# Weights split four units ahead, an input's own steps hurried alone, and new step numbers for a twelve-part transformer forward pass

## The chip, the cores and the metric

The kernel runs on one core of a Trainium2 chip. The metric is the time of one execution on the device in microseconds; of the kernel before, three runs gave 1786.06, 1789.84 and 1791.72 us, median 1789.84 us. TensorE does the matrix products, VectorE (DVE) and ScalarE (ACT) the element-wise work, GpSimd (POOL) a little of it, and SyncE (SP) issues nearly all DMAs.

## The reference, cut to what matters

The input is 256 tokens of 1024 float32 features. Four layers come first, each `x = x + m @ w_o` and then `x = x + ffn(rmsnorm(x))`, where m is an attention over `rmsnorm(x)`: differential attention in layers 0 and 3 (two softmaxes per head, subtracted, then a norm over the head's 128 features and a product with the values), stick-breaking attention in layer 1, sliding-window attention with sinks in layer 2. The feed-forward part is `(silu(gate) * val) @ w_down`, where gate and val come out of a 3-tap causal convolution over `h @ w_up`. A norm follows, and a second block: a SwiGLU feed-forward, a mixer (MoBA attention, which with 256 tokens is plain causal attention with ALiBi, beside a multi-scale pooling path), a cross-attention to 256 memory rows, and a second SwiGLU. Each branch of the second block is normed before and after:

```python
h = rmsnorm_2(x, mix_pre_g[l])
...
y = jnp.concatenate([attn, pool], axis=-1) @ w_out[l]
x = x + rmsnorm_2(y, mix_post_g[l])
```

## The kernel before, in words

**Weights.** All weight matrices lie in device memory as one stream in the order of use: blocks of 128x128, 8 blocks to a unit, two units to a 1 MB chunk, 564 units in all. SyncE loads a chunk into one of four `stage` buffers (`dma_to`, L124). A unit is split into a high part, rounded to the fast float32 format by ScalarE (`whi`, L162), and a low part, the rest, by VectorE (`wlo`, L165). There are five buffers for each part (`wsp`, L104). TensorE multiplies high weights by the high and by the low part of the input, and low weights by the high part: three matmuls of 256 columns to a block (`fm`, L187).

**The clock of the program is the block.** `self.pos` counts blocks. When `take` (L168) reaches the fifth block of unit u, it has the units up to u + AHEAD split, with AHEAD = 3 throughout (L115); the low part's instruction is issued `lag` blocks after the high part's. Everything that is not a weight product is a Python generator in `self.side` (`spawn`, L227). Each `yield n` puts its next step n blocks later, and `tick` (L231), called after every block, issues the steps that are due. The order in which the engines get their instructions is therefore written out by hand, in the numbers of `PLAN`, `MIX_PLAN`, `XA_STEPS`, `PACE`, `NORM_AT`, `V_AT`, `POST_AT`, `LAG` and `WARM`. Each engine works through its own instructions in that order and waits for the others by semaphores.

**Hurrying.** Where a weight product needs an input tile whose steps have not been issued yet (`kt not in act.done`, L191), it calls `tick(True)`, which issues the next step of every generator at once, whatever it belongs to, until the tile's steps are issued. `drain` (L239) does so until no generator is left.

**Attention layers** (`attn_layer`, L683). For each of 8 heads or blocks, q and k come from one unit each. `q_parts` and `k_parts` make the doubled high and low parts: a copy over 128x512 (L414, L433), and after `q[1]` or `k[1]` blocks the low parts on VectorE (L419, L437) and two copies over 64x256 (L438). The head's generator (`da_head`, `sb_block`, `sm_block`) starts `steps[0]` blocks after its k unit and then waits until both are issued (`parts_made`). The first numbers of `k` and `q` are the delay before the copy, `q_hi`, `k_hi` and `k_lo` say which engine copies (V or A). `out_proj` (L371) follows; the last head's steps are in `last`.

**Norms.** `feed` (L357) makes a tile of the next part's input (high part and square on ScalarE, low part and the sum of squares on VectorE). `start_norm` (L322) waits until all eight squares are summed, sums over partitions with a product by ones (L301), and makes 1/rms as `ln` and `exp` on ScalarE. The scale is applied to what comes out of the next weight product, so that product needs only the tiles of `feed`.

**Second block** (`body`, L1313). Between the first SwiGLU and the mixer stand 8 units that make the memory's keys (`mem_units(0, 8)`), 64 blocks, and beside them `post_apply` (L930) norms the branch, adds it to x and feeds the mixer's input tiles, one every PACE blocks from block POST_AT. Then comes `self.drain()` (L1357), and only then the mixer. The memory's values (`mem_units(8, 16)`, another 64 blocks) stand in the same way before the cross-attention. Before the second SwiGLU nothing stands between; 20 products of constants (`WARM`, L938) fill TensorE while the branch's norm is made.

Of the kernel before, what the change touches and what calls it, by code (L numbers as in the profile page):

```python
# [32 lines left out]
    dict(steps=(15, 7, 7, 2, 7, 4, 10, 2, 12, 11, 3), last=(9, 17, 5, 0, 1, 1, 6, 9, 5, 5, 7), q=(0, 2), k=(11, 5),  # L33
         q_hi="V", k_hi="A", k_lo="AA"),
    dict(steps=(14, 9, 3, 4, 4, 9, 2), last=(17, 8, 1, 8, 4, 9, 2), q=(2, 8), k=(2, 3), q_hi="A", k_hi="V", k_lo="AV"),
    dict(steps=(13, 8, 5, 4, 11, 8), last=(15, 8, 4, 0, 6, 2), q=(2, 8), k=(1, 8), q_hi="A", k_hi="A", k_lo="AA",
         norm="VVAA"),
    dict(steps=(14, 17, 9, 0, 9, 3, 9, 2, 9, 2, 7), last=(18, 7, 10, 1, 4, 0, 4, 11, 4, 1, 6), q=(2, 2), k=(3, 3),
         q_hi="A", k_hi="V", k_lo="AA"),
]  # L40
MIX_PLAN = dict(steps=(7, 13, 4, 6, 14, 1), last=(6, 17, 9, 10, 4, 7), norm="VVVV")
XA_STEPS = (0, 14, 2, 0)


PACE = dict(mix=10, xa=5, ffn2=6)
NORM_AT = (29, 11, 16, 10)
V_AT = (4, 5, 4, 6)
POST_AT = (3, 7)
LAG = (5, 7, 8, 6)
WARM = 20  # L50
# [42 lines left out]
class Net:  # L93
# [93 lines left out]
    def fm(self, specs, act, kts, first=True, last=True, rows=None, wide=False):  # L187
        ah, al = act.h, act.l
        for kt in kts:
            rw = rows[kt] if rows is not None else np.arange(128 * kt, 128 * kt + 128)  # L190
            while kt not in act.done:  # L191
                self.tick(True)
# [34 lines left out]
    def spawn(self, gen, delay=0):  # L227

        self.side.append([self.pos + delay, gen])

    def tick(self, force=False):  # L231
        for item in list(self.side):
            if item in self.side and (force or item[0] <= self.pos):
                try:
                    item[0] = self.pos + next(item[1])
                except StopIteration:
                    self.side.remove(item)
# [119 lines left out]
    def feed(self, act, j, g, split=True):  # L357
# [11 lines left out]
        self.spawn(low(), 1)  # L369
# [313 lines left out]
    def attn_layer(self, layer, xt):  # L683
# [4 lines left out]
        self.lag = LAG[layer]  # L688
        with ExitStack() as st:
# [9 lines left out]
            if mixer == 2:  # L699
# [7 lines left out]
                def block(b, ps):  # L707
# [3 lines left out]
                    self.spawn(self.sm_block(pool, oT, b, q, kk[b // 4], vget, sk, nxt, b == 7), plan[0])  # L711
# [8 lines left out]
            else:  # L720
# [17 lines left out]
                for h in range(8):  # L738
# [14 lines left out]
                    self.spawn(head, self.plan["last" if h == 7 else "steps"][0])  # L753
# [6 lines left out]
    def ffn_layer(self, layer, xf, nxt):  # L760
# [3 lines left out]
        with ExitStack() as st:  # L764
# [9 lines left out]
            self.lag = 6  # L774
            self.start_norm(delay=27)
# [47 lines left out]
            def start(n, i, bank, delay=0):  # L823
                gen = gate(n, i, bank)
                if delay:
                    self.spawn(gen, delay)
                else:
                    self.spawn(gen, next(gen))
# [34 lines left out]
    def swiglu(self, tag, xt, rget, down):  # L863

        nc = self.nc
        with ExitStack() as st:
# [36 lines left out]
            for i in range(22):  # L903
                if i < 2:
                    self.spawn(gate(i, lead[i]), 7 * i)
                else:
# [4 lines left out]
                    self.spawn(gen, next(gen))  # L911
# [549 lines left out]
```

## Time and profile before

| what | value |
|---|---|
| median of three runs | 1789.84 us |
| the profiled execution's own time | 1785.74 us |
| its span, first to last instruction | 1784.0 us |
| TensorE matmul busy | 1750.8 us (98%) |
| TensorE weight loads busy | 1636.8 us (92%) |
| VectorE busy | 1403.2 us (79%) |
| ScalarE busy | 1115.0 us (62%) |
| GpSimd busy | 27.1 us (2%) |
| mean granted TensorE clock over the span | 0.996 |

The busy time of a matmul is counted from its start to the modelled end of its way through the array, so neighbours overlap and a short wait between two of them hides in the overlap; a view that lists waits gives the part that is left over. Stages by time: start-up to 14 us, layer 0's attention to 143, its feed-forward part to 323, layer 1 to 628, layer 2 to 892, layer 3 to 1190, first SwiGLU to 1378, memory keys to 1402, mixer to 1492, memory values to 1515, cross-attention to 1580, second SwiGLU to the end.

### The profile page before, as it was taken

Reading aid. Unit: us, or ns where it says so; the run is one execution under the profiler, and the core shown is the slowest. Engines: PE = TensorE matmul, PEld = TensorE weight load, DVE = VectorE, ACT = ScalarE, POOL = GpSimd, SP = SyncE. Lnnn points to the kernel's source line nnn. Section 1 sums busy time; section 2 is a strip of 40 time slices with the busy share of each in tenths; the row PEclk is TensorE's granted clock in tenths of the full one; section 3 lists DMA queues with packets and bytes.
Section 4 is the critical chain, followed back from the end, with each engine's and each line's share of the span. In section 5 each row is a group of like instructions: output and inputs, shape, how many; then the busy total and the mean of one; then the engine's idle time right before and its main releaser. Section 6 shows DMA issues by size and latency. Waiting matters only on the chain.

```text
span 1784.0 us, 31555 instructions
## 1 busy us (share of the span) xinstructions
PE 1750.8 (98%) x12564; PEld 1636.8 (92%) x12564; DVE 1403.2 (79%) x2574; ACT 1115.0 (62%) x2004; POOL 27.1 (2%) x67
## 2 busy tenths in 40 slices
PE   8999999999999999999999999999999999999998
PEld 7899998999999899999899999988888889988886
DVE  6888996797998687998689799778865767558764
ACT  6676664676766477766467666556655456466653
POOL 1000000000000000000000000000000020000000
PEclk9999999999999999999999999999999999999999
DMA  8734555434455544455554355555555444345451
GB/s 276 253 136 169 190 186 200 155 142 164 156 190 201 198 154 165 149 189 187 201 189 151 146 189 190 189 195 182 190 189 189 166 154 166 120 153 186 172 212 68
DMA packets 56212, 314.66 MB, mean 176 GB/s; under 512 B 5616, under 2 KB 18320, under 8 KB 20224
## 3 DMA queue, kind: packets, MB, share of 16 engines
q1 hardware_dynamic: 54720, 309.79, 48.4%
q0 software_dynamic: 768, 2.09, 0.4%
q8 instruction: 99, 1.62, 0.4%
q10 hardware_dynamic: 576, 0.75, 0.1%
q14 instruction: 49, 0.40, 0.1%
HBM read 311.52 MB, written 5.29 MB: 178 GB/s over the span
## 4 chain that ended last, share of the span: by engine, by line
PE 79%; DVE 12%; ACT 5%; DMA 2%; issue 2%; DVEq 0%; ACTq 0%; SPq 0%
PE u L183 68%; PE s L183 10%; DVE wlo L165 3%; DMA stage<-w 1%; DVE y L797 1%; ACT whi L162 1%; DVE s L472 1%; ACT s L263 1%; DMA bt<-bt_d 1%; DVE qs L419 1%; PE s L489 0%; ACT ln L263 0%; DVE klow L437 0%; DVE u L886 0%; DVE u L883 0%
## 5 line engine op out<-in xcount | busy, mean ns | idle before, releaser
L183 PE MATMUL u<-xt,whi 128*128 128x256 f32 (+1 forms) x4352 | 863.0, 295 | 1.4 <-DVE xt L278 0.8
L165 DVE TENSOR_TENSOR wlo<-stage,whi 128x1024 fp32r<-128x1024 f32 (+1 forms) x568 | 680.3, 1213 | 73.1 <-ACT whi L162 72.1
L183 PEld LDWEIGHTS u<-xt,whi 128*128 128x128 f32 x4352 | 691.8, 192 | 21.2 <-issue 3.2
L183 PE MATMUL u<-xt,wlo 128*128 128x256 f32 x2352 | 666.1, 283 | 5.4 <-DVE wlo L165 5.4
L162 ACT ACTIVATE whi<-stage 128x1024 fp32r<-128x1024 f32 (+1 forms) x568 | 581.6, 1041 | 32.7 <-PE u L183 27.9
L183 PEld LDWEIGHTS u<-xt,wlo 128*128 128x128 f32 x2352 | 450.7, 192 | 7.0 <-DVE wlo L165 6.7
L183 PE MATMUL u<-ghl,whi 128*128 128x512 f32 x880 | 304.8, 389 | 0.0
L183 PE MATMUL u<-ghl,wlo 128*128 128x256 f32 x880 | 244.4, 279 | 0.0
L183 PEld LDWEIGHTS u<-ghl,whi 128*128 128x128 f32 x880 | 164.9, 187 | 37.8
L797 DVE SCALAR_TENSOR_TENSOR y<-ub,vec,y 128x256 f32<-128x256 f32 x344 | 159.5, 482 | 10.3 <-ACT y L793 3.3
L183 PEld LDWEIGHTS u<-ghl,wlo 128*128 128x128 f32 x880 | 165.0, 188 | 0.0
L183 PE MATMUL u<-o,whi 128*128 128x256 f32 x768 | 142.9, 286 | 0.1
L793 ACT ACTIVATE y<-ub,vec 128x256 f32<-128x256 f32 x172 | 94.2, 594 | 59.6 <-DVE ub L787 59.6
L183 PE MATMUL s<-xt,whi 128*128 128x512 f32 x352 | 128.1, 398 | 0.0
L183 PEld LDWEIGHTS u<-o,whi 128*128 128x128 f32 x768 | 118.7, 189 | 1.8 <-issue 1.2
L360 ACT ACTIVATE xt<-x,vec 128x256 fp32r<-128x256 f32 x72 | 36.4, 506 | 119.1 <-DVE x L846 89.9
L183 PE MATMUL u<-o,wlo 128*128 128x256 f32 x384 | 108.2, 282 | 0.0
L183 PE MATMUL s<-xt,wlo 128*128 128x256 f32 x352 | 99.9, 284 | 2.0 <-DVE wlo L165 1.7
L813 ACT ACTIVATE ghl<-g 128x256 fp32r<-128x256 f32 x88 | 36.9, 419 | 90.4 <-DVE g L809 88.5
L183 PE MATMUL u<-whi,xt 128*128 128x256 f32 (+1 forms) x448 | 90.0, 299 | 0.0
L263 ACT ACTIVATE s<-s,nm 128x128 f32<-128x128 f32 x112 | 49.7, 445 | 52.2 <-DVE nm L477 51.7
L183 PEld LDWEIGHTS s<-xt,whi 128*128 128x128 f32 x352 | 66.3, 188 | 15.5
(236 smaller groups left out, 2049.5 us busy)
## 6 DMA issues: line engine op xcount, KB each, us to landing
stage<-w SPq DMA_DIRECT2D x280, 1024.0 KB, 4.8
bt<-bt_d SPq DMA_DIRECT2D x24, 256.0 KB, 5.3
bt_d<-rows_d SPq DMA_DIRECT2D x1, 2048.0 KB, 12.3
stage<-w SPq DMA_DIRECT2D x4, 256.0 KB, 7.0
stage<-w SPq DMA_DIRECT2D x2, 512.0 KB, 9.0
bt_d<-rows_d SPq DMA_DIRECT2D x2, 512.0 KB
bt_d<-rows_d SPq DMA_DIRECT2D x1, 1024.0 KB
mem<-memT POOLq DMA_DIRECT2D x8, 128.0 KB, 2.6
```

Of the source, the lines that this page charges most:

```text
L162: nc.scalar.activation(hi[:, s], src[:, s], AF.Copy)
L165: nc.vector.tensor_tensor(lo[:, s], src[:, s], hi[:, s].bitcast(F32), OP.subtract)
L183: self.nc.tensor.matmul(out, lhsT, rhs, start=start, stop=stop, skip_group_check=True)
L263: self.nc.scalar.activation(out, in_, func, **kw)
L360: nc.scalar.activation(act.h[:, j], src, AF.Copy, scale=gcol)
L419: nc.vector.tensor_tensor(qs[other, j], q[own], qs[own, j].bitcast(F32), OP.subtract)
L472: nc.vector.tensor_tensor_reduce(s[:, j, sl], ps[j][:, sl], bt[:, j, bs], 1.0, init(j), OP.add, OP.max, mx[:, 2 * j + t:2 * j + t + 1])
L793: nc.scalar.activation(y[:, p], u[:, p, 2:258], AF.Identity, scale=cv(i, p, 2), bias=cv(i, p, 3))
L797: nc.vector.scalar_tensor_tensor(y[:, p], u[:, p, tap:tap + T], cv(i, p, tap), y[:, p], op0=OP.mult, op1=OP.add)
L813: nc.scalar.activation(gh[:m, i], g[:m], AF.Copy)
```

## The change: what it does

AHEAD becomes 4 in layers 1 to 3, in every feed-forward part and from there to the end; layer 0's attention keeps 3. A generator can be spawned with the input (`act`) that it makes, and where a product needs a tile of that input, `tick(act)` issues early the steps of that input's generators alone; the others stay at their due block. The two `drain` calls before the mixer and the cross-attention go, and `start_norm` gets a wait after the sums (0 and 4 blocks). The step numbers are new; layer 0's become nearly those of layer 3, including the engines of the two high copies.

```diff
 PLAN = [
-    dict(steps=(15, 7, 7, 2, 7, 4, 10, 2, 12, 11, 3), last=(9, 17, 5, 0, 1, 1, 6, 9, 5, 5, 7), q=(0, 2), k=(11, 5),
-         q_hi="V", k_hi="A", k_lo="AA"),
-    dict(steps=(14, 9, 3, 4, 4, 9, 2), last=(17, 8, 1, 8, 4, 9, 2), q=(2, 8), k=(2, 3), q_hi="A", k_hi="V", k_lo="AV"),
-    dict(steps=(13, 8, 5, 4, 11, 8), last=(15, 8, 4, 0, 6, 2), q=(2, 8), k=(1, 8), q_hi="A", k_hi="A", k_lo="AA",
-         norm="VVAA"),
-    dict(steps=(14, 17, 9, 0, 9, 3, 9, 2, 9, 2, 7), last=(18, 7, 10, 1, 4, 0, 4, 11, 4, 1, 6), q=(2, 2), k=(3, 3),
+    dict(steps=(14, 15, 11, 0, 9, 0, 9, 2, 9, 2, 12), last=(18, 7, 9, 1, 4, 1, 7, 11, 5, 1, 6), q=(2, 6), k=(5, 2),
+         q_hi="A", k_hi="V", k_lo="AA"),
+    dict(steps=(14, 9, 3, 7, 4, 9, 2), last=(17, 8, 1, 8, 4, 9, 2), q=(2, 8), k=(2, 5), q_hi="A", k_hi="V", k_lo="AV"),
+    dict(steps=(13, 8, 6, 4, 11, 8), last=(15, 8, 6, 0, 8, 2), q=(2, 8), k=(1, 8), q_hi="A", k_hi="A", k_lo="AA",
+         norm="VVAV"),
+    dict(steps=(14, 15, 11, 0, 9, 3, 9, 2, 9, 1, 12), last=(18, 7, 9, 1, 4, 0, 7, 11, 5, 1, 6), q=(2, 4), k=(6, 2),
          q_hi="A", k_hi="V", k_lo="AA"),
 ]
-MIX_PLAN = dict(steps=(7, 13, 4, 6, 14, 1), last=(6, 17, 9, 10, 4, 7), norm="VVVV")
-XA_STEPS = (0, 14, 2, 0)
-PACE = dict(mix=10, xa=5, ffn2=6)
-NORM_AT = (29, 11, 16, 10)
-V_AT = (4, 5, 4, 6)
-POST_AT = (3, 7)
-LAG = (5, 7, 8, 6)
-WARM = 20
+MIX_PLAN = dict(steps=(7, 13, 9, 7, 19, 1), last=(6, 17, 9, 10, 2, 7), norm="VVVV")
+R_WAIT = (0, 4)
+AHEAD = (3, 4, 4, 4)
+XA_STEPS = (0, 13, 3, 6)
+PACE = dict(mix=13, xa=8, ffn2=3)
+NORM_AT = (24, 12, 16, 11)
+V_AT = (6, 5, 4, 6)
+POST_AT = (4, 3)
+LAG = (9, 7, 8, 9)
+WARM = 12
...
             while kt not in act.done:
-                self.tick(True)
+                self.tick(act)
...
-    def spawn(self, gen, delay=0):
-        self.side.append([self.pos + delay, gen])
+    def spawn(self, gen, delay=0, act=None):
+        self.side.append([self.pos + delay, gen, act])
     def tick(self, force=False):
         for item in list(self.side):
-            if item in self.side and (force or item[0] <= self.pos):
+            if item in self.side and (force is True or item[0] <= self.pos or force and item[2] is force):
...
-        self.spawn(low(), 1)
+        self.spawn(low(), 1, act)
...
         self.lag = LAG[layer]
+        self.AHEAD = AHEAD[layer]
...
             self.lag = 6
+            self.AHEAD = 4
...
-                self.spawn(self.post_apply(xm, "mix_pre_g_2", PACE["mix"]), POST_AT[0])
-                self.start_norm(0.125, True)
+                self.spawn(self.post_apply(xm, "mix_pre_g_2", PACE["mix"]), POST_AT[0], xm)
+                self.start_norm(0.125, True, wait=R_WAIT[0])
                 self.mem_units(0, 8)
-                self.drain()
...
-                self.spawn(self.post_apply(xx, "xa_pre_g_2", PACE["xa"]), POST_AT[1])
-                self.start_norm(1.0 / 16)
+                self.spawn(self.post_apply(xx, "xa_pre_g_2", PACE["xa"]), POST_AT[1], xx)
+                self.start_norm(1.0 / 16, wait=R_WAIT[1])
                 self.mem_units(8, 16)
-                self.drain()
...
-            self.spawn(self.post_apply(xl, "ffn2_pre_g_2", PACE["ffn2"], True))
+            self.spawn(self.post_apply(xl, "ffn2_pre_g_2", PACE["ffn2"], True), 0, xl)
```

The heads, the gates of the feed-forward parts and the pooling groups are spawned with their own input in the same way.

## Rows read from the trace of the kernel before

**Rows 1.** Waits by engine, whole span: total us, times, longest us.

```profile
PE u L183 <- DVE wlo L165: 5.4, 5, 1.2
ACT whi L162 <- PE u L183: 27.9, 18, 2.4
```

**Rows 2.** Weight loads' waits, whole span, same columns.

```profile
PEld s L183 <- DVE wlo L165: 4.4, 8, 1.2
```

**Rows 3.** Busy us of engines in stretches: PE, PEld, DVE, ACT, POOL; clock; DMA.

```profile
30.00:143.00 113.00, 106.15 (x845) 102.85 (x844) 95.42 (x248) 77.13 (x179) 0.17 (x3) 1.00 0.59 207
892.00:1010.00 118.00, 117.58 (x955) 115.86 (x955) 100.92 (x251) 84.35 (x190) 0.16 (x3) 1.00 0.47 167
...
160.00:180.00 20.00, 20.00 (x169) 20.00 (x168) 19.30 (x33) 13.59 (x22) 0.00 (x0) 1.00 0.54 193
...
1240.00:1260.00 20.00, 19.44 (x108) 16.26 (x107) 16.75 (x30) 13.72 (x28) 0.54 (x1) 1.00 0.57 199
```

**Rows 4.** TensorE's waits in layer 0's attention, 30 to 143 us.

```profile
PE s L183 <- ACT ks L403: 3.8, 6, 0.9
PE s L183 <- DVE klow L437: 3.0, 4, 1.2
```

**Rows 5.** Chain that ended last, in order of time: start us, us, what.

```profile
42.59 12.94 DMA bt<-bt_d
```

**Rows 6.** VectorE in order of time, start of layer 0's feed-forward part.

```profile
152.25 1.21 DVE L165 TENSOR_TENSOR wlo<-stage,whi 128x1024 fp32r<-128x1024 f32 x1
...
156.61 1.22 DVE L165 TENSOR_TENSOR wlo<-stage,whi 128x1024 fp32r<-128x1024 f32 x1
```

**Rows 7.** TensorE's waits, 1190 to 1378 us (first SwiGLU).

```profile
PE s L183 <- DVE wlo L165: 1.7, 5, 0.9
```

**Rows 8.** TensorE's waits, 1378 to 1415 us, before the mixer.

```profile
PE s L183 <- DVE accss L295: 2.8, 1, 2.8
PE s L351 <- ACT r L263: 1.0, 1, 1.0
```

**Rows 9.** VectorE in order of time beside the memory keys: one round.

```profile
1389.36 0.41 DVE L943 TENSOR_TENSOR f<-f,r 128x256 f32<-128x256 f32 x1
1389.81 0.42 DVE L944 TENSOR_TENSOR x<-x,f 128x256 f32<-128x256 f32 x1
1390.15 0.48 DVE L364 SCALAR_TENSOR_TENSOR xt<-x,vec,xt 128x256 fp32r<-128x256 f32 x1
1390.55 0.41 DVE L295 TENSOR_TENSOR accss<-accss,sq 128x256 f32<-128x256 f32 x1
1390.88 1.22 DVE L165 TENSOR_TENSOR wlo<-stage,whi 128x1024 fp32r<-128x1024 f32 x1
1392.02 0.41 DVE L1055 TENSOR_TENSOR mK<-u,r 128x256 f32<-128x256 f32 x1
```

**Rows 10.** Engines in stretches, columns as in Rows 3.

```profile
1407.00:1410.30 3.30, 3.30 (x17) 3.30 (x18) 2.19 (x3) 2.18 (x3) 0.00 (x0) 0.51 0.00 0
1584.20:1587.20 3.00, 2.93 (x10) 2.48 (x11) 2.02 (x6) 2.06 (x4) 0.00 (x0) 0.56 0.00 0
```

**Rows 11.** In order of time, before the mixer: ones product, then scales.

```profile
1405.18 0.70 PE L183 MATMUL s<-accss,ones 128*128 128x256 f32 x2 [2.78 <-DVE accss L295]
...
1406.87 0.42 ACT L333 ACTIVATE rq<-r 128x256 f32<-128x256 f32 x1
```

**Rows 12.** TensorE's waits, 1495 to 1523 us, before the cross-attention.

```profile
PE s L183 <- DVE accss L295: 1.2, 1, 1.2
```

**Rows 13.** TensorE in order of time, before the second SwiGLU.

```profile
1580.92 2.53 PE L183 MATMUL s<-ones_r 128*128 128x128 f32 x20
1584.27 0.56 PE L183 MATMUL u<-xt,whi 128*128 128x512 f32 x1 [0.81 <-DVE xt L278]
```

**Rows 14.** Groups of instructions by form, layer 2, 628 to 711 us.

```profile
L633 ACT ACTIVATE s<-s,rs 128x256 f32<-128x256 f32 x8 | 4.0, 502 | 0.0
L635 DVE TENSOR_SCALAR s<-s,rs 128x256 f32<-128x256 f32 x8 | 2.8, 348 | 0.0
```

More of the change, by code (lines that the diff above doesn't have):

```diff
@@ L710, in block @@
                     plan = self.plan["last" if b == 7 else "steps"]
-                    self.spawn(self.sm_block(pool, oT, b, q, kk[b // 4], vget, sk, nxt, b == 7), plan[0])
+                    self.spawn(self.sm_block(pool, oT, b, q, kk[b // 4], vget, sk, nxt, b == 7), plan[0], oT)
                 rows = [np.concatenate([np.arange(64 * h, 64 * h + 64) for h in SW_HEADS[b]]) for b in range(8)]
@@ L752, in attn_layer @@
                         pool, oT, h, q, k, vget)
-                    self.spawn(head, self.plan["last" if h == 7 else "steps"][0])
+                    self.spawn(head, self.plan["last" if h == 7 else "steps"][0], oT)
                     if h // 2 not in vs and h in (0, 2, 4, 7):
@@ L824, in start @@
                 gen = gate(n, i, bank)
[L825 to L828, printed above, removed]
+                self.spawn(gen, delay or next(gen), ga)
             self.fm([(b[:, p * T:p * T + T], name, layer, cols, p == 0)
@@ L904, in swiglu @@
                 if i < 2:
-                    self.spawn(gate(i, lead[i]), 7 * i)
+                    self.spawn(gate(i, lead[i]), 7 * i, ga)
                 else:
@@ L910, in swiglu @@
                     gen = gate(i, outs)
-                    self.spawn(gen, next(gen))
+                    self.spawn(gen, next(gen), ga)
             down(ga)
@@ L1028, in finish @@
                 while kt not in act.done:
-                    self.tick(True)
+                    self.tick(act)
                 if h == 0 or kt < 18:
@@ L1103, in mix @@
                 p, q, k = self.units("w_in_2", 0, [1536 + c, c, 512 + c], xt)
-                self.spawn(self.pool_group(pool, oT, b, p))
+                self.spawn(self.pool_group(pool, oT, b, p), 0, oT)
                 q = self.scaled(pool, q, self.rq, "q", 3)
@@ L1107, in mix @@
             else:
-                self.spawn(self.pool_group(pool, oT, b, self.unit("w_in_2", 0, 1536 + c, xt)))
+                self.spawn(self.pool_group(pool, oT, b, self.unit("w_in_2", 0, 1536 + c, xt)), 0, oT)
                 q = self.scaled(pool, self.unit("w_in_2", 0, c, xt), self.rq, "q", 3)
@@ L1111, in mix @@
             plan = self.plan["last" if b == 3 else "steps"]
-            self.spawn(self.sm_block(pool, oT, b, q, k, vget, None, nxt, b == 3), plan[0])
+            self.spawn(self.sm_block(pool, oT, b, q, k, vget, None, nxt, b == 3), plan[0], oT)
             if b % 2:
@@ L1160, in xa @@
             q = [self.scaled(pool, p, self.rq, "q", 5) for p in ps]
-            self.spawn(self.xa_head(pool, oT, h, q), XA_STEPS[0])
+            self.spawn(self.xa_head(pool, oT, h, q), XA_STEPS[0], oT)
     def prelude(self, small):
```

## The prediction, made before the result was known

> **What bounds the kernel now.** I read the waits of TensorE first, because its matmuls are busy for 98% of the span: what the change can win is what TensorE waits for, and the list is short. The largest entries by place are low weight parts that come late, five times, 5.4 us [rows 1]; the same in the first SwiGLU's second bank, where the weight loads show 4.4 us [rows 2]; the parts of k in layer 0's attention, 6.8 us [rows 4]; and the norm before the mixer, 3.8 us [rows 8]. The stretches came next. In layer 3's attention TensorE is busy for 117.58 of 118 us, in layer 0's, with the same kind of heads, for 106.15 of 113 [rows 3]: layer 0 has idle time that layer 3 has not. In the middle of a feed-forward part 169 matmuls fill 20 us [rows 3], so a matmul of 256 columns takes 0.118 us and a block of three 0.355 us; I turn steps into time with that. There TensorE is at its pace and no order of steps helps.
>
> **The change part by part.** *AHEAD 4 in the feed-forward parts.* A split now takes the place that the previous unit's split had in the queues of ScalarE and VectorE, 8 blocks or 2.8 us earlier. At the start of layer 0's feed-forward part the low part that TensorE waits for begins at 156.61; the split one place earlier began at 152.25 [rows 6], 4.4 us before, and the wait is 1.1 to 1.2 us. So one place covers it. There is one such wait in each of the four convolution parts and a smaller one in the second SwiGLU, together the 5.4 us of [rows 1]. VectorE's work stays the same, so what is late next is the split after it, with the same lead. I take 5.0 us off, between 2 and 5.4.
>
> In the first SwiGLU the waits repeat: 1.7 us in TensorE's list [rows 7], 4.4 us in that of the weight loads [rows 2], in which the overlap with the matmul before is not hidden. VectorE is busy there for 16.75 of 20 us [rows 3], not full, so this is a backlog and not a rate, and 2.8 us more lead covers most of it. I take 3.0 us, about the middle, between 0 and 4.4.
>
> What this edit adds is a wait. Five buffers hold the high parts; a split four units ahead needs the buffer of the unit just finished, that is, TensorE must have come to 4 blocks before the split's place in the order, where it was 12 before. Behind the split in ScalarE's queue stand evacuations, gates and the copies of the heads, and VectorE waits for those. Today 18 of the 564 splits wait for TensorE, 27.9 us in all [rows 1], on an engine that is idle for a third of the span. I cost the edit at 0, because what stands behind a split mostly needs a product that is issued at about the same block; if that cover is missing it is the slow rival below. The loads of chunks are also queued by the splits, 8 blocks earlier on SP, and still wait for a stage buffer.
>
> *Layer 0's steps.* Now k's low parts are issued 16 blocks after k, and the scores right behind them, so TensorE arrives while ScalarE and VectorE are still copying: 3.8 and 3.0 us [rows 4]. With k=(5, 2) they are issued 7 blocks after k and the scores after 14: 7 blocks, 2.5 us, against 0.9 and 1.2 us for the longest waits. The two high copies trade engines, one each, so neither engine gets more. Against the full 6.8 us stands head 2's bias table: its load starts at 42.59 and takes 12.94 us [rows 5], so its scores can't be used before 55.5 us, whatever TensorE does; and VectorE is busy for 95.42 of 113 us [rows 3], so a gain in the first heads is partly given back. LAG 9 for 5 puts the low parts 4 blocks (1.4 us) later, and SP, which waits for them before it loads a chunk, holds the bias tables behind it. I take 4.0 us, between a loss of 1.4 and a gain of 6.8. The norm of layer 0, 5 blocks earlier, costs nothing as long as the sums are there.
>
> *The mixer's start.* Today the drain puts all eight feeds before the mixer; TensorE waits 2.8 us for the sums and 1.0 us for the scale [rows 8], and then runs at a granted clock of 0.51, the 1.2 GHz level, for 3.3 us: 17 matmuls, which at 0.118 us are 2.0 us, so 1.3 us lost [rows 10]. Together 5.1 us. After: in the 64 blocks of the memory keys, feeds at 4, 17, 30, 43 and 56 make five of eight. The three left are issued as the mixer's first three units (p, q, k; 3 blocks to a tile, 1.07 us) ask for them. On VectorE a tile costs 0.41+0.42+0.48+0.41 = 1.72 us [rows 9] and three eighths of a split of 1.22 us, 2.2 us in all, so 1.1 us short per tile, 3.3 us for three. Tiles 0 to 4 give 5.3 us of TensorE work, in which VectorE does two splits (2.4 us) and gets some 2.9 us ahead, not all of it usable, since the high parts queue behind splits on ScalarE: a wait of 1.0 us. Then the norm: from the ones product to the end of the scale is 1405.18 to 1407.29 [rows 11], and q must leave its bank (0.4 us) before the next unit can begin, as all three banks are taken; 2.5 us, less one block of 0.36: 2.1 us. 5.1 - 3.1 = 2.0 us won, between a loss of 1 (all 3.3 us paid, and the clock falls again) and a gain of 3.8.
>
> *The cross-attention's start.* The wait for the sums is 1.2 us [rows 12]; with four blocks (1.4 us) between the sums and the product and no drain, 1.0 us goes, between 0 and 1.2.
>
> *The second SwiGLU's start.* The 20 products take 2.53 us, and after them TensorE still waits 0.81 us for the input tile [rows 13]. Twelve end 1.0 us earlier and the tile comes when it came. The clock is granted at 0.56 in the 3 us after that, 20 products or not [rows 10]; one such stretch more or less is about 1.5 us, and I take 0. The Trainium skill, page "TensorE: Matmul & The Clock Gate", section "What's actually happening", says that the throttled clock is the default and that activity releases it; that speaks against fewer filler products, and by it the sum would be 1776.3 us instead of 1774.8. This trace doesn't bear out that the 20 help.
>
> *The rest.* Hurrying only an input's own steps keeps splits and other heads at their place; at the end of the attention layers the last heads' steps are few, and nothing is listed there. In layer 2 one norm of eight blocks goes from ScalarE (502 ns) to VectorE (348 ns) [rows 14]. With the new numbers of layers 1 to 3, mixer and cross-attention: 0, give or take 1 us.
>
> *Sum.* 5.0 + 3.0 + 4.0 + 2.0 + 1.0 = 15.0 us. The profiled execution took 1785.74 us, which gives 1770.7; the median of the timed runs lies 4.1 us above it, so 1774.8.
>
> **The rivals.** *VectorE and the loads take it back.* Layer 0 stays bound by the bias table and VectorE, the first SwiGLU's backlog eats the longer lead, and the mixer pays for its three late tiles. Then 5.0 + 1.0 = 6.0 us are left: 1783.8. For it: VectorE's 84% in layer 0. Against it: 86% in layer 3 without waits [rows 3].
>
> *The change doesn't do what it says.* Each wait goes one place on (the split after, the scores after), since the same engines do the same work. Gain about 1: 1788.8. Against it speaks that the waits are single ones behind bursts, five in 564 units.
>
> *The split stops ScalarE's queue.* Place: the 132 gates of the six feed-forward parts. A split that waits for the unit just finished holds the gate's activations behind it, the bank is freed late, and TensorE waits for the bank. Price: 0.2 us a gate, a fraction of the 2.8 us by which the buffer now comes later, is 26.4 us: 1801.2, slower. It decides from 0.11 us a gate, where 15.0 us are eaten. For it: splits wait for TensorE already [rows 1]. Against it: only 18 do, and no wait for a bank stands among TensorE's in those parts. The same page, section "Architectural detail: the array is 16× 32×32, not 1× 128×128", says that ScalarE and VectorE take their instructions strictly in order and TensorE alone pulls weight loads ahead; by that rule what is behind a waiting split waits too. No row here shows a case against it.
>
> **How the numbers follow.** Forecast 0.70 (own range 1767 to 1782); taken back 0.15; nothing done 0.08; ScalarE stopped 0.07. A measurement of this kernel tells about 0.3% from no change, 5.4 us, so the line is at 1784.5: the forecast lies below it, of the second case about half. Faster 0.78, same 0.15, slower 0.07. With all upper bounds the gain is 6.8+5.4+4.4+3.8+1.2 = 21.6 us, with 1.5 for the clock 23: 1766.7. With the lower ones it is -1.4+2+0-1+0-1.5 = -2: 1791.7. The range that leaves out two in ten: 1765 to 1788.
>
> **What would show it.** Right: no entry for `wlo` in TensorE's waits after layer 0, `ks` and `klow` under 1 us, a start of the mixer with two waits of 1 and 2 us. Wrong: waits of TensorE for a bank (`ub`, `u` L883), longer waits of ScalarE's `whi` for TensorE with gates late behind them, or head 2's table landing after 55.5 us and layer 0's attention as long as before.

## The result, and the profile after

The changed kernel takes 1764.11 us (median of four runs, 1761.36 to 1765.8) against 1788.18 us for the kernel before beside it: ratio 0.9864, 95% interval 0.9848 to 0.9881. It is faster by 24.1 us, where I forecast 15.0; the time lies 0.9 us below the low end of my range. The profiled execution took 1761.36 us, its span is 1759.6 us. The direction and most of the mechanisms were right, several sizes were not: between the two profiled spans lie 24.4 us, and 4.5 of the 9.4 us by which these exceed the forecast stand in one term, the mixer's start.

TensorE's list of waits, whole span of the changed kernel (us in total, times, longest), answers to [rows 1, 4 and 8]; the row of ScalarE is from the same view:

```profile
ACT whi L164 <- PE u L185: 69.4, 56, 1.9
...
PE s L185 <- DMA oh<-onehot: 2.6, 1, 2.6
PE s L185 <- ACT osq L541: 2.0, 1, 2.0
PE u L185 <- DVE xt L281: 1.7, 1, 1.7
PE s L185 <- DVE eps L1197: 1.1, 1, 1.1
PE s L185 <- DVE qs L422: 1.0, 1, 1.0
PE u L185 <- DVE q L654: 0.9, 1, 0.9
...
PE u L185 <- DVE wlo L167: 0.4, 2, 0.2
```

Late low parts (`wlo`) fell from 5.4 us to 0.4; `ks`, `klow`, `accss` (before the mixer and, [rows 12], before the cross-attention) and `r` are gone; new in their places are `osq` in layer 0 and `q` at the mixer's start. ScalarE's high parts now wait 69.4 us for TensorE instead of 27.9 [rows 1], and no entry of TensorE's list answers to that; one in the list of the weight loads does, see u_ahead. What is left of `wlo`, 0.4 us, lies in the first SwiGLU, for the 1.7 of [rows 7]. The weight loads, same columns, for [rows 2]:

```profile
PEld u L185 <- DVE wlo L167: 1.1, 2, 0.5
```

Engines in stretches (columns as in [rows 3]): layer 0's attention, layer 3's, the middle of a feed-forward part, the first SwiGLU.

```profile
30.00:138.00 108.00, 105.85 (x847) 104.21 (x847) 96.27 (x249) 78.49 (x180) 0.17 (x3) 0.98 0.61 214
900.00:1010.00 110.00, 109.80 (x893) 108.48 (x892) 93.94 (x232) 79.73 (x179) 0.17 (x3) 1.00 0.47 165
160.00:180.00 20.00, 20.00 (x169) 20.00 (x169) 19.30 (x34) 13.59 (x23) 0.00 (x0) 1.00 0.53 201
1230.00:1250.00 20.00, 19.55 (x111) 16.58 (x110) 16.76 (x31) 13.73 (x27) 0.54 (x1) 1.00 0.47 168
```

Layer 0 does about the same products (847 matmuls, 845 before) in 108 us where it took 113. The feed-forward part's middle is still 169 matmuls in 20 us: there was nothing to win, as forecast.

To see where the 24.4 us between the two spans went, I cut each trace where a stage's last weight product starts (us; L0 counts from the span's start, FFN is each of the four feed-forward parts, G1 the first SwiGLU, F2 the second):

```text
            L0     FFN     L1      L2      L3      G1     keys  mixer values cross    F2
before    132.78 186.40  115.67   80.23  112.64  190.45  24.76  90.09  24.84  62.77  197.64
after     127.36 185.00  115.70   81.20  111.99  186.62  24.41  83.94  23.20  62.11  196.54
u_ahead   126.77 186.40  115.32   80.93  111.65  189.40  24.41  83.83  22.98  62.10  195.67
a_ahead   139.05 185.00  116.03   80.74  112.95  186.59  24.77  91.03  24.84  62.77  196.55
u_layer0  132.12 185.00  115.71   81.23  111.98  187.62  24.40  83.96  22.98  62.11  196.45
u_drain   126.24 185.00  115.70   81.25  111.98  186.62  24.76  88.78  24.87  61.68  196.43
u_mixsteps 125.89 185.00 115.70   81.25  111.98  187.62  24.40  85.23  23.20  63.22  196.28
u_hurry   131.23 185.00  115.70   81.27  112.55  186.59  24.41  83.95  23.20  62.12  194.91
u_layer2  127.32 185.00  115.70   80.60  111.99  187.60  24.42  83.97  22.97  62.11  196.55
b_osq     128.70 185.00  115.71   81.21  111.99  186.61  24.41  83.96  22.98  62.10  196.56
c_drains  126.69 185.00  115.70   81.25  111.98  187.63  24.40  91.42  22.97  63.43  197.16
c_pace    133.35 185.00  115.70   81.25  111.98  186.62  24.77  83.93  24.85  61.68  197.18
c_warm    129.82 185.00  115.70   81.30  111.99  186.62  24.40  83.97  22.98  62.11  197.15
d_table   124.79 185.00  115.70   80.62  111.98  187.63  24.41  83.98  22.98  62.11  197.16
```

The other rows are the experiments below. From L1 to the cross-attention a stage whose steps are untouched mostly repeats within 0.3 us, so a single profile tells an edit's price there to some tenths; G1 comes as 186.6 or 187.6, layer 0 and F2 vary more. Where a stall brings the half clock it is less exact: in a_ahead the mixer's start has the waits of the kernel before (2.8 and 1.0 us), but half clock for about 6.8 us in place of 3.3, and the mixer is 0.9 us longer. Some expectations below count stages from one norm's product with ones to the next; the change shifts these by up to 4 blocks (1.4 us), so I read them in this table.

The mixer's start in the changed kernel, TensorE in order of time (start us, us, line, matmul, count, wait), answers to [rows 11]:

```profile
1392.97 0.40 PE L185 MATMUL u<-xt,whi 128*128 128x256 f32 x2
...
1394.06 0.42 PE L185 MATMUL u<-xt,whi 128*128 128x256 f32 x2
...
1394.80 0.40 PE L185 MATMUL u<-xt,whi 128*128 128x256 f32 x2
...
1395.16 0.70 PE L185 MATMUL s<-accss,ones 128*128 128x256 f32 x2
1395.51 0.59 PE L185 MATMUL u<-xt,whi 128*128 128x256 f32 x2
...
1396.65 0.28 PE L185 MATMUL u<-xt,wlo 128*128 128x256 f32 x1
1397.79 0.50 PE L185 MATMUL u<-xt,whi 128*128 128x256 f32 x2 [0.86 <-DVE q L654]
```

The last three tiles cost nothing, the product with ones comes without a wait, and one wait for the bank of q is left. VectorE beside it, in order of time (in brackets its own wait):

```profile
1389.99 0.48 DVE L367 SCALAR_TENSOR_TENSOR xt<-x,vec,xt 128x256 fp32r<-128x256 f32 x1
...
1391.63 1.23 DVE L167 TENSOR_TENSOR wlo<-stage,whi 128x1024 fp32r<-128x1024 f32 x1 [0.82 <-ACT whi L164]
...
1393.57 0.48 DVE L367 SCALAR_TENSOR_TENSOR xt<-x,vec,xt 128x256 fp32r<-128x256 f32 x1
1393.96 0.42 DVE L298 TENSOR_TENSOR accss<-accss,sq 128x256 f32<-128x256 f32 x1
1394.30 0.48 DVE L367 SCALAR_TENSOR_TENSOR xt<-x,vec,xt 128x256 fp32r<-128x256 f32 x1
1394.69 0.42 DVE L298 TENSOR_TENSOR accss<-accss,sq 128x256 f32<-128x256 f32 x1
```

Each tile has three blocks of weight products, so TensorE reaches the last three tiles at 1392.97, 1394.06 and 1395.51. Their low parts (`xt`) end at 1390.47, 1394.05 and 1394.78: the first is early by 2.5 us, the second comes just in time, and so does the last sum, which ends at 1395.11 for the product with ones at 1395.16. VectorE even idles 0.82 us on the way.

### The profile page after: what moved, and what is told of

Its sections match the earlier page's. It is cut to its first block, busy times and chain, and to the rows that moved or that the text cites. A ratio compares the mean times of both kernels' runs of the same rounds, so it can differ in the third digit from the quotient of the medians.

```text
span 1759.6 us, 31591 instructions
## 1 busy us (share of the span) xinstructions
PE 1742.1 (99%) x12556; PEld 1635.2 (93%) x12556; DVE 1404.4 (80%) x2582; ACT 1118.0 (64%) x1996; POOL 27.4 (2%) x67
## 4 chain that ended last, share of the span: by engine, by line
PE 92%; DVE 5%; ACT 2%; issue 1%; DMA 0%; POOL 0%; DVEq 0%; ACTq 0%; POOLq 0%
PE u L185 80%; PE s L185 11%; DVE wlo L167 1%; DVE s L475 1%; PE s L492 1%; DMA oh<-onehot 0%; ACT s L266 0%; ACT whi L164 0%; DVE u L888 0%; DVE u L885 0%; ACT mt L280 0%; DVE mt L281 0%; POOL ps L1080 0%; DVE qs L422 0%; DVE s L638 0%
## 5 line engine op out<-in xcount | busy, mean ns | idle before, releaser
L164 ACT ACTIVATE whi<-stage 128x1024 fp32r<-128x1024 f32 (+1 forms) x568 | 586.9, 1043 | 82.4 <-PE u L185 69.4
## 6 DMA issues: line engine op xcount, KB each, us to landing
bt_d<-rows_d SPq DMA_DIRECT2D x1, 2048.0 KB, 12.2
```

What stands on the lines that cost most here:

```text
L164: nc.scalar.activation(hi[:, s], src[:, s], AF.Copy)
```

## The experiments

My theory was that each term is a separate saving by its own edit. The rivals were that one edit carries the whole, or that a wait only moves on. Those named u_ undo one part of the changed kernel each.

**u_ahead: three units ahead again.**

```diff
-AHEAD = (3, 4, 4, 4)
+AHEAD = (3, 3, 3, 3)
...
-            self.AHEAD = 4
+            self.AHEAD = 3
```

> The changed kernel with the weights again split three units ahead everywhere. Theory (the lead took away the late low parts): the waits for wlo come back, about 1.1 us at the start of each of the four convolution parts, several in the first SwiGLU, one in the second; those stages grow by what they had lost against the kernel before (4.9 us in the four, 3.8 us in the first SwiGLU, about 1 us in the second), so 9 to 10 us in all: 1773 to 1774 us. Rival (hurrying an input's own steps alone is what keeps the low parts in time): under 2 us, 1764 to 1766.

Measured: 1770.83 us, ratio to the kernel before 0.9908 (0.9882 to 0.9934). TensorE's waits, whole span:

```profile
PE u L185 <- DVE wlo L167: 4.6, 4, 1.2
...
PE s L185 <- DVE wlo L167: 1.3, 3, 0.8
```

The late low parts are back, in the four convolution parts and the first SwiGLU; the one in the second SwiGLU is not, and that stage is 0.9 us shorter in this profile, in which no half clock fell there, not 1 us longer. In the table each feed-forward part is longer by 1.40 us, the first SwiGLU by 2.78. The fourth unit ahead is worth 8.4 us there and costs 0.38, 0.27 and 0.34 us in layers 1, 2 and 3, 1.0 us in all; the total stays below the 1773 to 1774 that I expected. The price stands in the list of the weight loads of the changed kernel, and not in that of u_ahead:

```profile
PEld u L185 <- DVE x L399: 0.9, 3, 0.3
```

It is one wait for a bank in each of the three output products. Layer 1's, ScalarE and then VectorE in order of time, changed kernel:

```profile
419.29 1.06 ACT L164 ACTIVATE whi<-stage 128x1024 fp32r<-128x1024 f32 x1 [1.86 <-PE u L185]
```

```profile
420.38 1.23 DVE L167 TENSOR_TENSOR wlo<-stage,whi 128x1024 fp32r<-128x1024 f32 x1 [1.33 <-ACT whi L164]
421.53 1.41 DVE L399 TENSOR_TENSOR x<-x,u 128x256 f32<-128x256 f32 x4
```

The high part waits 1.86 us for a buffer that TensorE still uses, VectorE waits 1.33 us for that high part, and the additions to x that free the banks stand behind the low part on VectorE. Layers 2 and 3 show the same order, with 1.78 and 1.21 us on ScalarE. So the waiting split reached TensorE through VectorE.

**a_ahead: the kernel before with the fourth unit ahead alone, from layer 1 on and in every feed-forward part.**

```diff
         self.lag = LAG[layer]
+        self.AHEAD = 4 if layer else 3
...
             self.lag = 6
+            self.AHEAD = 4
```

> The kernel before with the splits four units ahead from layer 1 on and nothing else. Theory (the lead alone): no wlo in TensorE's waits, 9 to 10 us off, 1778 to 1779 us; the waits before the mixer and in layer 0 stay as they were. Rival (ScalarE's queue stopped by the splits, hidden in the whole change by other gains): 5 us or less off, with longer waits behind whi.

Measured: 1777.18 us, ratio 0.9952 (0.9937 to 0.9967). Each feed-forward part took 185.00 us (1.40 less), the first SwiGLU 186.59 (3.86 less), layers 1 to 3 0.36, 0.51 and 0.31 us more. No `wlo` is left in TensorE's list. The edit does alone what it does in company. Layer 0, whose steps are those of before here, took 139.05 us in this profile, which the edit doesn't touch: SyncE's loads landed late, ScalarE waited 5.6 us for a weight chunk and TensorE 5.4 us for `ks` behind it (more on late loads: d_table).

**u_layer0: layer 0's steps of before.**

```diff
-    dict(steps=(14, 15, 11, 0, 9, 0, 9, 2, 9, 2, 12), last=(18, 7, 9, 1, 4, 1, 7, 11, 5, 1, 6), q=(2, 6), k=(5, 2),
-         q_hi="A", k_hi="V", k_lo="AA"),
+    dict(steps=(15, 7, 7, 2, 7, 4, 10, 2, 12, 11, 3), last=(9, 17, 5, 0, 1, 1, 6, 9, 5, 5, 7), q=(0, 2), k=(11, 5),
+         q_hi="V", k_hi="A", k_lo="AA"),
...
-NORM_AT = (24, 12, 16, 11)
-V_AT = (6, 5, 4, 6)
+NORM_AT = (29, 12, 16, 11)
+V_AT = (4, 5, 4, 6)
...
-LAG = (9, 7, 8, 9)
+LAG = (5, 7, 8, 9)
```

> The changed kernel with layer 0's steps, norm time, value delay and lag of the kernel before. Theory (the scores came right behind k's copies): layer 0 from start to the norm after its attention grows by the 5.4 us that it lost, to 143 us, ks and klow stand again in TensorE's waits with 6 to 7 us, and the stretch at half clock near 59 us goes: 1769.5 us. Rival (the bias table and VectorE bound layer 0, and the gain came from elsewhere): under 2 us.

Measured: 1767.74 us, ratio 0.9896 (0.9872 to 0.992). Layer 0's waits, 14 to 150 us:

```profile
PE s L185 <- ACT ks L406: 3.2, 6, 0.8
PE s L185 <- DVE klow L440: 2.9, 5, 1.2
```

They are back, 3.2 and 2.9 us for the 3.8 and 3.0 of [rows 4], the half clock near 59 us is gone, and layer 0 is 4.8 us longer than in the changed kernel.

**u_drain: both drains, the paces, the starts and the wait after the sums of before.**

```diff
-R_WAIT = (0, 4)
+R_WAIT = (0, 0)
...
-PACE = dict(mix=13, xa=8, ffn2=3)
+PACE = dict(mix=10, xa=5, ffn2=3)
...
-POST_AT = (4, 3)
+POST_AT = (3, 7)
...
                 self.mem_units(0, 8)
+                self.drain()
...
                 self.mem_units(8, 16)
+                self.drain()
```

> The changed kernel with the two drains, the pace, start and norm waits before the mixer and the cross-attention as in the kernel before; MIX_PLAN and XA_STEPS stay new. The stretch from the first product of the memory keys to the end of the mixer shrank by 7.9 us, where 2.0 were forecast. Theory A (the drain's idle time and the half clock behind it were that gain, and the wait left over was overestimated): 5 to 6 us more there and 1 us before the cross-attention, 1770 to 1771 us, with a stretch at half clock after the drain. Theory B (the new step numbers inside the mixer carry it): 2 to 3 us more, 1766 to 1767.

Measured: 1770.38 us, ratio 0.9901 (0.9879 to 0.9923). Keys and mixer together are longer by 5.2 us, values and cross-attention by 1.2. The waits of [rows 8] are back with 2.8 and 1.0 us, and half clock follows them.

**c_drains: the two drains alone.**

```diff
                 self.mem_units(0, 8)
+                self.drain()
...
                 self.mem_units(8, 16)
+                self.drain()
```

> The changed kernel with the two drain calls put back and nothing else: paces, starts and the wait after the sums stay as changed. With all four undone, the stretch from the memory keys to the mixer's norm had grown by 6.6 us (109.4 to 116.0). Theory (the drain is what cost: with it no product of the mixer can begin before all eight input tiles and the norm's square root are there): with the slower pace of 13, more tiles are late than before, so the loss is as large or larger: stretch +6 to +9 us, a wait of TensorE for the sum accss or the scale r of 3 us or more, half clock again at the mixer's start, total 1770 to 1774. Rival (the pace and the early start of the tiles did it, the drain merely stands there): stretch +0 to +2 us, total 1764 to 1766. Cross-attention: +0 to +1 us in either.

**c_pace: the other half of u_drain, without the drains.**

```diff
-R_WAIT = (0, 4)
+R_WAIT = (0, 0)
...
-PACE = dict(mix=13, xa=8, ffn2=3)
+PACE = dict(mix=10, xa=5, ffn2=3)
...
-POST_AT = (4, 3)
+POST_AT = (3, 7)
```

> The changed kernel with the tiles' paces (10 and 5), their starts (3 and 7) and the wait after the sums (0) of the kernel before; the drains stay out. Theory (the drain is what cost): memory keys and mixer stay within 1 us of the changed kernel's 109.4 us, total 1763 to 1766. Rival (the pace did it): stretch +4 us or more, total 1768 or more. By my forecast's own sum for the start (three tiles of the changed kernel late by 1.0 us in all, the scale by 2.1) a pace that has seven tiles done instead of five would win about 1 us: stretch -1 us.

Measured: c_drains 1770.44 us, ratio 0.9913 (0.9886 to 0.9939); c_pace 1767.34 us, 0.9886 (0.9863 to 0.9909). The ten us after the last product of the memory keys (columns as in [rows 3]), first in the kernel before, then in the changed kernel, then in c_drains:

```profile
1402.20:1412.20 10.00, 6.21 (x36) 5.61 (x35) 5.41 (x11) 4.59 (x8) 0.00 (x0) 0.83 0.51 187
```

```profile
1387.40:1397.40 10.00, 9.53 (x76) 9.10 (x74) 8.14 (x16) 6.73 (x13) 0.00 (x0) 1.00 0.71 242
```

```profile
1387.80:1397.80 10.00, 4.57 (x21) 3.85 (x20) 5.80 (x14) 3.97 (x8) 0.00 (x0) 0.75 0.33 119
```

36 matmuls before, 76 after, 21 with the drains and the new pace, and where few run the clock is granted at 0.83 and 0.75. c_drains in order of time:

```profile
1387.65 0.28 PE L185 MATMUL u<-mt,wlo 128*128 128x256 f32 x1
1392.34 0.90 PE L185 MATMUL s<-accss,ones 128*128 128x256 f32 x2 [4.41 <-DVE accss L298]
1394.25 0.69 PE L354 MATMUL s<-ident,r 128*128 128x128 f32 x2 [1.01 <-ACT r L266]
```

So the theory held at the mixer: the drain alone makes it 7.5 us longer, the pace without it 0.0 (and the keys 0.4). The pace of 13 is right only where no drain waits for the tiles: with one, it leaves three tiles to be made while TensorE stands still. Of the 2.6 us by which c_drains' mixer is longer than u_drain's, 1.6 are the longer wait (4.4 us against 2.8); about 6.8 us of half clock behind it in place of 3.3 are the likely rest. Values and cross-attention together are longer by 1.2 us with the old pace, start and wait, by 1.1 with the drain and by 1.2 with both, so these prices don't add. The total of c_pace lies above what the theory named: its edits account for 1.6 us, and in the profiled execution (1769.58 us) layer 0 is 6.0 us longer, 133.35 us, which none of them touches. The other runs of c_pace have no profile.

**u_mixsteps: the mixer's and the cross-attention's steps of before.**

```diff
-MIX_PLAN = dict(steps=(7, 13, 9, 7, 19, 1), last=(6, 17, 9, 10, 2, 7), norm="VVVV")
+MIX_PLAN = dict(steps=(7, 13, 4, 6, 14, 1), last=(6, 17, 9, 10, 4, 7), norm="VVVV")
...
-XA_STEPS = (0, 13, 3, 6)
+XA_STEPS = (0, 14, 2, 0)
```

> The changed kernel with MIX_PLAN and XA_STEPS of the kernel before. Theory A: 1 to 2 us more, in the mixer (waits for s at L638 and for the transposes come back), 1765 to 1766 us. Theory B (the step numbers carry most of the 7.9 us): 4 to 5 us more, 1768 to 1769.

Measured: 1764.32 us, ratio 0.9881 (0.9853 to 0.9909). Mixer 1.3 us longer, cross-attention 1.1. TensorE's waits show what came back in the mixer's transposes:

```profile
PE s L492 <- DVE s L638: 0.9, 2, 0.5
```

The steps of the second block, which I had put under "the rest" at 0, are worth 2.4 us. In the median it does not show against the changed kernel; the stages show it.

**u_hurry: hurrying everything again.**

```diff
-                self.tick(act)
+                self.tick(True)
```

> The changed kernel with every generator hurried where a tile is missing, as in the kernel before. Theory (hurrying the rest only moves single steps at the ends of the attention layers and at the mixer's start): within 2 us, 1763 to 1766 us; at the mixer's start the three late tiles then push other steps forward, at most 1 us more there. Rival (keeping the others in place is a part of the gain that I left out): 3 us or more, 1767 or above, spread over the four output products.

Measured: 1762.51 us, ratio 0.9864 (0.985 to 0.9879). Layer 3 is 0.6 us longer, the rest from L1 to the cross-attention the same; F2 is 1.6 shorter, but no half clock came there in this profile, and in the others it did or didn't with F2 between 195.7 and 197.2. TensorE's list has two waits of 0.7 us that the changed kernel lacks, both for the last head's tile of `o` (L553), in layer 0 and in layer 3. Beyond these, no saving by hurrying an input's own steps alone can be told, and the timed runs show none.

**u_layer2: layer 2's steps of before.**

```diff
-    dict(steps=(13, 8, 6, 4, 11, 8), last=(15, 8, 6, 0, 8, 2), q=(2, 8), k=(1, 8), q_hi="A", k_hi="A", k_lo="AA",
-         norm="VVAV"),
+    dict(steps=(13, 8, 5, 4, 11, 8), last=(15, 8, 4, 0, 6, 2), q=(2, 8), k=(1, 8), q_hi="A", k_hi="A", k_lo="AA",
+         norm="VVAA"),
```

> The changed kernel with layer 2's steps of the kernel before (fourth norm on ScalarE again). Layer 2's attention is the one stage that grew, by 1.0 us. Theory (VectorE got the fourth norm where it was full): layer 2 shrinks by 1 us, 1763 us, and the wait for qs falls from 1.0 to about 0.5 us. Rival (it grew by the longer lead, ScalarE held by its splits): no change in layer 2.

Measured: 1759.89 us, ratio 0.9847 (0.9831 to 0.9864). Layer 2 is 0.6 us shorter: those numbers were a loss. The wait for `qs` fell from 1.0 to 0.5 us, as named, and one of 0.5 us for `o` (L606) went; which of the numbers did it is not shown. The stages explain 0.6 us, not the 4.2 between the medians.

**b_osq: layer 0, other steps between the scores and `osq`.**

```diff
-    dict(steps=(14, 15, 11, 0, 9, 0, 9, 2, 9, 2, 12),
+    dict(steps=(14, 15, 7, 0, 6, 0, 13, 2, 9, 2, 12),
```

> The changed kernel with layer 0's heads multiplying by the values 7 blocks earlier, so that head 0's square stands before head 2's exponentials on ScalarE. Theory (TensorE's 2.0 us for osq near 55.5 us and the half clock after it come from head 2's bias table, which holds VectorE and then ScalarE): both go, layer 0 shrinks by 3 to 4 us, 1760 to 1761 us. Rival (VectorE is behind anyway and the wait moves to the low parts or the scores): under 1 us.

Measured: 1763.38 us, ratio 0.987 (0.9854 to 0.9886). Layer 0's waits, 14 to 145 us:

```profile
PE s L185 <- ACT aT L530: 3.9, 4, 1.3
PE s L185 <- DVE accss L298: 0.8, 1, 0.8
```

The wait for `osq` went and one for `aT` came; layer 0 took 128.70 us, inside the spread of the changed steps. The wait moved. VectorE began head 2's scores at 53.5 us here, as in u_drain, where layer 0 took 126.24: beside that these steps lose 2.5 us.

**d_table: head 2's bias table loaded earlier in layer 0, and layer 2's steps of before.**

```diff
...
         self.bts[1] = self.load_bias(pool, 0, (2, 3))
         self.toeplitz(0, 4, 8)
-        yield 24
+        yield 12
+        self.bts[2] = self.load_bias(pool, 0, (4, 5))
+        yield 12
...
-        if h + 2 < 8:
+        if h + 2 < 8 and h + 2 not in self.bts:
```

> The changed kernel with layer 2's step numbers of before, and head 2's bias table of layer 0 loaded by bias_tables, 12 blocks after head 1's, instead of behind head 0's scores: some 7 us earlier in SyncE's queue. Theory (that table's late landing is what makes TensorE wait 2 us in layer 0 and then run at half clock): no wait of VectorE for bt, no wait of TensorE for osq, no half clock near 59 us, layer 0's attention 134 to 136 us instead of 137.5; layer 2 84.0 us; total 1756 to 1760. Rival (SyncE then waits for the table's source in device memory, and the weight chunks behind it come late): a wait of TensorE or of the splits for a stage buffer between 30 and 50 us, layer 0 138 us or more, total 1761 or more.

Measured: 1759.3 us, ratio 0.9843 (0.9822 to 0.9864). Layer 0 took 124.79 us, less than in any of the nine profiles with the same steps and the late table. Among those nine its length follows that table: VectorE begins head 2's scores at 53.2, 54.1, 55.6, 56.5 and 60.4 us, and layer 0 takes 125.89, 127.36, 129.82, 131.23 and 133.35 us (u_mixsteps, the changed kernel, c_warm, u_hurry, c_pace). The other four, with 53.5 to 54.1 us and 126.24 to 127.32, lie in the same order, though u_hurry's length has a wait of its own in it. In each of the nine the scores begin 0.1 us after the table has landed, by the trace. What VectorE waits for before it adds the tables, 30 to 75 us, c_pace:

```profile
  DMA bt<-bt_d: 7.8, 1
```

In d_table that view has no such entry, and TensorE's waits are:

```profile
PE s L185 <- ACT osq L541: 0.7, 1, 0.7
PE s L185 <- DVE accss L298: 0.7, 1, 0.7
```

Of the wait for `osq` 0.7 us is left, where I expected none. From 59 to 62.5 us the clock is granted at 1.00 there. So the rival fell, though SyncE issued nothing from 34.3 to 40.40 us, when it issued the table: ScalarE's wait for a chunk between 28 and 52 us is 1.9 us, 1.8 in the changed kernel. The timed runs don't tell it from u_layer2 (1759.3 and 1759.89). Both are the fastest kernels of the study, but their intervals overlap that of the changed kernel, and that they beat it by 4 us is not shown.

**c_warm: twenty products of constants again.**

```diff
-WARM = 12
+WARM = 20
```

> The changed kernel with 20 products of constants in place of 12 before the second SwiGLU. Theory (they only fill a wait that the input tile sets): TensorE's wait for xt falls from 1.7 to about 0.8 us, the second SwiGLU's stage stays within 0.3 us of 202.9 us where the half clock comes and of 201.3 to 202.7 where it does not, total 1763 to 1765. Rival (more activity keeps the clock up): no stretch at a granted clock of 0.5 behind them, stage 201.3 us or less, total 1761 to 1763.

Measured: 1763.24 us, ratio 0.9866 (0.9838 to 0.9894). The start of the second SwiGLU, first in the changed kernel, then in c_warm:

```profile
1557.65 1.64 PE L185 MATMUL s<-ones_r 128*128 128x128 f32 x12
1561.00 0.80 PE L185 MATMUL u<-xt,whi 128*128 128x512 f32 x1 [1.71 <-DVE xt L281]
```

```profile
1559.98 2.53 PE L185 MATMUL s<-ones_r 128*128 128x128 f32 x20
1563.33 0.50 PE L185 MATMUL u<-xt,whi 128*128 128x512 f32 x1 [0.81 <-DVE xt L281]
```

The first product comes 3.35 us after the first filler with twelve and with twenty. The clock right behind (columns as in [rows 3]), changed kernel, then c_warm:

```profile
1561.00:1564.30 3.30, 3.30 (x10) 2.81 (x11) 2.08 (x6) 2.27 (x4) 0.00 (x0) 0.50 0.50 211
```

```profile
1563.30:1566.60 3.30, 3.27 (x11) 2.85 (x12) 2.08 (x6) 2.27 (x4) 0.00 (x0) 0.57 0.55 231
```

Mostly half clock with either count, as in [rows 10]; the wait grew with fewer fillers by what they took less, 0.81 us as in [rows 13] or 1.71. Over all profiles the half clock came there in 8 of 11 with twelve fillers (not in u_hurry, u_mixsteps and u_ahead) and in 2 of 3 with twenty (not in a_ahead). F2 is 0.6 us longer than in the changed kernel, where I had said 0.3 at most. The rival fell.

## Why the prediction was right or wrong

**The mixer's start: the step that failed.** I wrote "5.1 - 3.1 = 2.0 us won", with 3.8 as the most, and put the steps of the mixer at nothing. Keys and mixer together gained 6.5 us. Four sizes were wrong.

- What stood there before: I took the 3.8 us of [rows 8] and 1.3 for the clock. The list counts from the modelled end of a matmul. From start to start, the last key product at 1402.12 us and the mixer's first at 1407.10, it is 4.98 us; less a step of 0.12 and 0.35 for the product with ones, which the changed kernel pays too, 4.5 are lost, with the clock's 1.3 it is 5.8. So 0.7 too few.
- What would be left: I had 1.0 us for three late tiles and 2.1 for the scale. From start to start, 1396.65 to 1397.79 us, less a step, it was 1.0. My sum made all three tiles wait for the mixer's units to ask for them. But the tiles' generator keeps its own pace: the first of the three was due 71 blocks after the start of the keys, 7 into the mixer, and ScalarE makes its high part at 1388.46 us, before the split that the mixer's second unit issues (1390.54); only two were hurried, and these came just in time. And three blocks of weight products, not one, stood behind the product with ones. So 2.1 too many.
- The keys got 0.35 us shorter by the slower pace (c_pace gives it back).
- The mixer's own steps are worth 1.3 us (u_mixsteps); I had them at 0, although a wait of 0.8 us for VectorE in its transposes stood in the list of before:

```profile
PE s L489 <- DVE s L635: 0.8, 2, 0.5
```

2.0 + 0.7 + 2.1 + 0.35 + 1.3 = 6.45, against 6.5 in the table. The undoing runs agree: 5.2 (u_drain) and 1.3 (u_mixsteps).

**The feed-forward parts and the first SwiGLU.** Right in the main. Forecast 5.0 and 3.0; four times 1.40 is 5.6, and u_ahead gives the SwiGLU 2.8. My 5.0 counted the second SwiGLU's wait in; it went in a_ahead and did not come back in u_ahead, so the fourth unit is not all that keeps it away. That the first SwiGLU fell by 3.8 includes 1.0 us that comes and goes between profiles of the same code: it builds up evenly over some 50 us in the middle, in u_layer2 as in the kernel before, and not in the changed kernel or u_ahead. No wait is listed for it, and I leave it open.

**Layer 0.** Forecast 4.0, profile 5.4, by undoing 4.8. One profile on either side says little of the size here: the changed steps took 125.89 to 133.35 us in nine profiles, the old ones 132.12, 132.78 and 139.05. `ks` and `klow` went as forecast. The bias table, which I had named as what would stand against the full gain, does: TensorE waits 2.0 us for `osq`, because the exponentials of head 2's late scores stand before it on ScalarE. The chain in order of time (start us, us):

```profile
54.77 0.20 DVE s L475
...
55.62 1.86 ACT s L266 x8
57.49 0.28 ACT osq L541
...
57.81 0.70 PE s L185 x2
```

Behind the wait the clock falls, at 59.10 us in the changed kernel:

```profile
59.10:62.40 3.30, 3.30 (x17) 3.21 (x16) 3.16 (x9) 3.19 (x7) 0.00 (x0) 0.50 0.02 9
```

17 matmuls take 3.3 us there instead of 2.0, by the 0.118 us of a matmul: that is 1.3 us (1.5 by comparing matmul for matmul with u_mixsteps, where the clock stayed full), and my forecast had no place for it.

**The cross-attention.** Forecast 1.0, measured 2.3: the start gave 1.2 (u_drain) and the steps 1.1 (u_mixsteps), which I had at 0.

**The second SwiGLU's start.** Forecast 0, stage 1.1 us shorter, but F2 took 194.9 to 197.2 us in profiles of the same or nearly the same code, so nothing is shown. Its pace of 3 was not undone alone. The rule that I weighed from the Trainium skill's "TensorE: Matmul & The Clock Gate", "What's actually happening", would have made the fewer fillers cost 1.5 us; no run here bears it out: the fillers' number changed neither the first product's time nor the half clock.

**The rest.** Layers 1 to 3 lost 0.35 us in sum: the fourth unit ahead costs 1.0, layer 2's steps 0.6, and hurrying an input's own steps alone gains 0.6 in layer 3; another 0.7 us or so of gain lies in step numbers that were not undone alone. I had 0, give or take 1.

5.6 + 3.8 + 5.4 + 6.5 + 2.3 + 1.1 - 0.35 = 24.35 us, against 24.4 between the spans.

**The rivals.** "VectorE and the loads take it back" and "doesn't do what it says" would have left the waits in place; they are gone. "The split stops ScalarE's queue" was right in its first half alone: high parts wait 41.5 us longer for TensorE. In the changed kernel no bank of a gate is late in TensorE's list. The price is the 1.0 us in the output products of layers 1 to 3, against 26.4; there a bank was late, not behind ScalarE's queue but behind the low part on VectorE. I had the edit's price at 0.

**The range.** I put 3.8 as the most for the mixer's start and 0 for the steps of the second block. With what these gave (5.2, and 2.4) the upper bounds, 23 us then, give 26.8, and the range reaches to 1763.

## What to carry to other kernels

Read a stall of TensorE from start to start in the order of time, and add the slow clock behind it: the list of waits gave 3.8 us where 5.8 were lost. A barrier in the order of issue costs the whole latency of what it waits for, and taking it out changes which pace is best on both sides, so price the two together, not each against the old other. A split that waits for a buffer costs little where its engine has idle time and what stands behind it is not due yet: here 41.5 us more of such waits cost TensorE 1.0, and the place to look for it was the engine that uses the split's result.

## What the runs showed of the hardware

In layer 0, listed waits for `osq` of 1.8 to 2.1 us (the changed kernel, u_ahead, u_layer2, c_drains) were followed by about 3.3 us at a granted clock of 0.50, the 1.2 GHz level, and with those of 3.7, 4.3 and 7.9 us (c_warm, u_hurry, c_pace) came about 6.8, which began before the wait was over; after 0.7 to 1.1 us (d_table, u_mixsteps, u_drain) the clock stayed at 1.00. The same wait does not always bring the same: before the mixer 2.8 and 1.0 us brought 3.3 us of it in the kernel before and in u_drain, 6.8 in a_ahead, and before the second SwiGLU 1.7 us brought 0.50 in the changed kernel and 1.00 in u_hurry.

A 256 KB table that stood on SyncE's queue behind 1 MB chunks and a 1 MB copy of tables within device memory (`bt_d<-rows_d`) landed after 7.9 to 12.9 us in the changed kernel and 12.2 to 18.4 in c_pace, with the same order of loads. In d_table, where head 2's table was issued ahead of that copy, it landed after 3.8 us. Which of the loads before it held it is not shown. The spread moves layer 0 by several us.
